# Part "a11 less a21" of a down projection, split twice: seven half-width products in place of four full ones

## The chip, the cores and the metric

One core of one Trainium2 chip runs the kernel. The metric is the device time of one execution in microseconds (us), the median over runs of the same kernel. TensorE (PE) multiplies matrices, VectorE (DVE) and ScalarE (ACT) work on elements, POOL and SP here mostly issue transfers: each has one queue of its own.

## The reference

One layer of a residual block over 2048 frames of 1024 channels: a mixer (pooling branch, convolution branch, gates, output projection) and then an MLP with a squared ReLU, everything in float32. The change touches the MLP's second product, `w_down`, and when its sums are made:

```python
D_MODEL, SEQ, D_FF = 1024, 2048, 4 * 1024
def rmsnorm(x, g):
    y = x * lax.rsqrt(jnp.mean(x * x, axis=-1, keepdims=True) + EPS)
    return y * g
...
    merged = jax.nn.sigmoid(g_a) * branch_a + jax.nn.sigmoid(g_b) * branch_b
    x = x + rmsnorm(merged @ w_o[l], norm_mix_post[l])
    h = rmsnorm(x, norm_mlp_pre[l])
    f = jnp.square(jax.nn.relu(h @ w_up[l])) @ w_down[l]
    x = x + rmsnorm(f, norm_mlp_post[l])
```

## The kernel before, in words

**Numbers in two parts.** TensorE multiplies values rounded to a shorter form (`fp32r`). So every operand is split (`split`, `parted`): ScalarE makes the high part, a rounded copy; VectorE makes the low part, the value minus that copy. A product is high by high, high by low, low by high. Weights go through `wr` (as loaded) or `ws` (a sum) to `wh` and `wl`; cells (tiles of activations, 128 x 1024 floats, 512 KB) get their parts in tiles named `big` and `tr`. `product` multiplies one weight tile with two cells in 24 matmuls of 128 x 512. In each row of them the low part of the first cell is needed at the second matmul, that of the second cell at the sixth, and the low weight at the seventh.

**Seven products for eight.** Each large product is made by a Strassen-like scheme: the two factors are cut in two by two, and seven products of sums of the pieces (numbered 1 to 7) replace eight. For the down projection parts 1, 2 and 4 have a plain piece of the weight, 3, 5, 6 and 7 a sum of pieces; part 7 has the weight a11 less a21 (blocks 0 and 2 of `w_down`). Parts 1 and 2 are cut in the same way a second time and so cost 14 half products of 24 matmuls each; the others are plain: eight jobs (s, i, b), slab s of four, token half b of two, two products of 24 each, 48 matmuls.

**The order of the down projection** (`jobs`, `items`): part 1 in seven level products (`level_product`), then part 5, part 6, part 3, part 7, part 2 in 14 halves (`level_half`), part 4, and a tail (`at_end`) with the last norm. One job of part 7, `FILL`, is made early as a filler while the output projection ends, and its result is fetched and added later. `last_product` adds a plain part's finished products into the results `c01`, `c11`, `c00` and `u`, kept in tiles `big`; four `Finish` objects take their squares and gains as the results become ready.

**What sets the order.** The program is written in the order of TensorE's work, and a compiler's list scheduler places the other engines' instructions by it. `behind()` ties what is written inside it behind the work that stands there; `tc.high_priority(offset=AHEAD)` moves it ahead. The resulting order of each engine's rows is fixed when the program is built: at run time each engine takes its rows in that order and waits where a row isn't ready. Work beside the main line is written as generators in a `Lane`, which takes so many steps of it (its rate) at each `bg()`, after each product. Two matter here. In up's second block a lane forms the weight sums of part 1's second level (`level_weights`) and then the MLP norm's squares and roots (`scales`). From the first job of part 3 on (`PREPARE`) a lane forms part 2's weight sums and cell sums (`level_weights(2, 1)`, `level_cells`); it stores them by POOL's queue (`aside`), and SP's queue (`load`) brings them back. `empty()` runs out what is left of all lanes at once.

## Time and profile before

| | before |
|---|---|
| runs | 2161.08, 2161.93, 2154.96 us; median 2161.08 |
| profiled execution | 2162.05 us, its span 2160.3 us |
| granted clock of TensorE, mean | 0.997 |
| busy: PE, DVE, ACT, POOL | 2137.6, 1688.5, 1045.0, 78.1 us |
| filler | about 1228 to 1239 us from the span's start |
| up, second block | about 1241 to 1558 us |
| part 1 (7 level products) | about 1558 to 1634 us |
| parts 5, 6, 3 | about 1634 to 1722, to 1809, to 1897 us |
| part 7 (7 jobs) | about 1897 to 1973 us |
| part 2 (14 halves) | about 1973 to 2050 us |
| part 4 | about 2050 to 2146 us |

The stages are read from the timeline of TensorE by the names of the tiles that it writes and the engines' busy time from the page's first part. A stage's windows give for each engine the busy time and, in brackets, the number of instructions; then the granted clock, the DMA engines' share and GB/s. Some matmul records are missing, so counts in a window are a few below those of the program.

### The profile page before, as it was taken

How to read it: one execution, taken by the hardware profiler on the slowest of the kernel's cores; microseconds unless marked ns; L12 is line 12 of the kernel's file. 1: busy time of each engine (PE TensorE's matmuls, PEld its weight loads, DVE VectorE, ACT ScalarE, POOL GpSimd, SP SyncE). 2: the span in 40 equal slices, each digit the busy share in tenths (PEclk: the TensorE clock that was granted, in tenths of full speed). 3: DMA queues.
4: the chain of work that ended last, by engine and by line, in shares of the span. 5: the costliest groups of instructions: out<-in, count | busy, mean ns of one | idle time of the engine just before them, and what ended most of it. 6: DMA issues, size and time to landing. Idle time of an engine off the chain costs nothing.

```text
span 2160.3 us, 25332 instructions
## 1 busy us (share of the span) xinstructions
PE 2137.6 (99%) x9585; PEld 1769.7 (82%) x9585; DVE 1688.5 (78%) x1655; ACT 1045.0 (48%) x1094; POOL 78.1 (4%) x143
## 2 busy tenths in 40 slices
PE   9999999999999999999999999999999999999998
PEld 7888888888888888888888878888888888888887
DVE  8997789998688998987858784776776657576975
ACT  6444454334543545545644674655663332234761
POOL 1000000000000000000000000000000000120002
PEclk9999999999999999999999999999999999999999
DMA  7688898777997787545787698577697997896877
GB/s 272 243 293 315 326 352 283 253 255 290 340 369 251 253 333 278 193 166 195 289 308 288 238 358 329 212 257 285 258 374 302 348 381 259 336 365 238 299 258 208
DMA packets 173930, 618.40 MB, mean 286 GB/s; under 512 B 19312, under 2 KB 21616, under 8 KB 173808
## 3 DMA queue, kind: packets, MB, share of 16 engines
q1 hardware_dynamic: 143168, 506.44, 64.4%
q0 software_dynamic: 17824, 64.07, 8.4%
q10 hardware_dynamic: 12816, 46.27, 5.5%
q8 instruction: 75, 1.23, 0.2%
q14 instruction: 47, 0.39, 0.1%
HBM read 406.89 MB, written 209.81 MB: 285 GB/s over the span
## 4 chain that ended last, share of the span: by engine, by line
PE 80%; issue 8%; DVE 6%; DMA 5%; ACT 1%; SPq 0%; POOL 0%; DVEq 0%; POOLq 0%; ACTq 0%
PE down L268 20%; PE up L268 19%; PE wo L268 8%; PE ga L268 7%; PE gb L268 7%; PE glu L268 5%; PE B L268 4%; PE rb L268 4%; PE A L268 3%; PE pool L268 3%; DVE big L121 1%; DMA fo<-w_down 1%; DVE y L1002 1%; DMA big<-fd 1%; DMA big<-x1d 1%
## 5 line engine op out<-in xcount | busy, mean ns | idle before, releaser
L268 PE MATMUL up<-big,wh 128*128 128x512 f32 x1792 | 482.7, 391 | 4.7 <-DVE big L121 2.9
L268 PEld LDWEIGHTS up<-big,wh 128*128 128x128 f32 x1792 | 337.2, 188 | 77.0 <-DVE big L121 4.1
L225 ACT CAST wh<-wr 128x1024 fp32r<-128x1024 f32 x196 | 205.9, 1051 | 308.4 <-PE up L268 90.3
L1002 DVE SCALAR_TENSOR_TENSOR y<-v,cst,y 128x1024 f32<-128x1024 f32 x240 | 307.3, 1281 | 2.8
L268 PE MATMUL down<-big,wh 128*128 128x512 f32 x872 | 295.4, 390 | 0.8 <-DVE big L121 0.8
L268 PE MATMUL up<-big,wl 128*128 128x512 f32 x896 | 277.8, 391 | 0.0
L225 ACT CAST wh<-ws 128x1024 fp32r<-128x1024 f32 x128 | 134.5, 1052 | 273.5 <-PE up L268 65.8
L268 PE MATMUL down<-big,wl 128*128 128x512 f32 x688 | 212.1, 389 | 0.0
L268 PEld LDWEIGHTS up<-big,wl 128*128 128x128 f32 x896 | 169.1, 189 | 35.1
L268 PE MATMUL down<-tr,wh 128*128 128x512 f32 x504 | 196.2, 389 | 0.5 <-DVE tr L121 0.5
L268 PEld LDWEIGHTS down<-big,wh 128*128 128x128 f32 x872 | 163.6, 188 | 35.3 <-DVE big L121 1.1
L121 DVE TENSOR_TENSOR wl<-ws,wh 128x1024 fp32r<-128x1024 f32 x120 | 146.5, 1221 | 58.5 <-ACT wh L225 58.1
L121 DVE TENSOR_TENSOR wl<-wr,wh 128x1024 fp32r<-128x1024 f32 (+1 forms) x121 | 146.3, 1210 | 28.2 <-ACT wh L225 27.8
L121 DVE TENSOR_TENSOR big<-big,big 128x1024 fp32r<-128x1024 f32 (+1 forms) x108 | 129.6, 1220 | 37.6 <-ACT big L1137 13.8
L121 DVE TENSOR_TENSOR tr<-tr,big 128x1024 fp32r<-128x1024 f32 x94 | 112.7, 1220 | 54.2 <-ACT big L1864 41.7
L268 PEld LDWEIGHTS down<-big,wl 128*128 128x128 f32 x688 | 129.1, 188 | 26.8
L268 PE MATMUL wo<-big,wh 128*128 128x512 f32 x480 | 128.5, 390 | 0.0
L268 PE MATMUL glu<-big,wh 128*128 128x512 f32 x464 | 125.3, 391 | 1.3 <-ACT big L796 0.8
L1864 ACT CAST big<-tr 128x1024 fp32r<-128x1024 f32 x70 | 72.0, 1048 | 100.0 <-DMA tr<-fd 76.7
L268 PE MATMUL gb<-big,wh 128*128 128x512 f32 x448 | 120.0, 390 | 0.0
L268 PE MATMUL ga<-big,wh 128*128 128x512 f32 x448 | 119.9, 389 | 0.0
L268 PEld LDWEIGHTS down<-tr,wh 128*128 128x128 f32 x504 | 94.6, 188 | 20.6 <-DVE tr L121 1.0
(240 smaller groups left out, 3431.6 us busy)
## 6 DMA issues: line engine op xcount, KB each, us to landing
tr<-fd SPq DMA_DIRECT2D x98, 512.0 KB, 7.8
wl<-kept SPq DMA_DIRECT2D x85, 512.0 KB, 5.0
wr<-w_down SPq DMA_DIRECT2D x80, 512.0 KB, 7.3
kept<-wl SPq DMA_DIRECT2D x72, 512.0 KB, 6.0
wr<-w_up SPq DMA_DIRECT2D x64, 512.0 KB, 4.8
wr<-w_in SPq DMA_DIRECT2D x59, 512.0 KB, 5.5
fd<-tr ACTq DMA_DIRECT2D x54, 512.0 KB, 3.9
big<-fd SPq DMA_DIRECT2D x48, 512.0 KB, 7.1
```

Source lines behind the costliest of these rows:

```text
L121: return nc.vector.tensor_tensor(o, a, b, op=ALU.subtract)
L225: nc.scalar.copy(hi[:, :n], src[:, :n])
L268: i = nc.tensor.matmul(ps, w[wp][:, (at + k) * P : (at + k + 1) * P], rhs[k][xp], start=start and n == 0, stop=stop and n == len(order) - ...
L1002: nc.vector.scalar_tensor_tensor(acc, v[:, k : k + TB], wk, acc, op0=ALU.mult, op1=ALU.add)
L1864: nc.scalar.copy(hi, t)
```

## The change

Part 7 is split a second time, as parts 1 and 2 are. Its eight jobs become 14 halves (`halves(7)`), which stand between part 6 and part 3; the order is now part 1, 5, 6, 7 (halves), 3, 2 (halves), 4. `level_half` adds their sums into `u`, and when one is complete, `u` into `c11`. The filler becomes a job of part 4. The weight sums of part 7's second level are formed by `level_weights_7`, 16 sums, in the lane of up's second block, ahead of `scales`, at rate 1.2; each loads two blocks of `w_down` by POOL's queue and stores the kept ones likewise. The cell sums are formed by `level_formed` during parts 5, 6 and the halves themselves, with loads by SP's queue. `PREPARE` stays at part 3's first job, but part 3 is now followed at once by part 2's halves, where `empty()` runs its lane out. On the whole VectorE has 40 rows more, ScalarE 16 casts more, SP's queue 10 transfers more and POOL's 34, and TensorE 48 matmuls fewer.

```diff
         kept_as(3, a12)
         yield
 
+    def level_weights_7(n):
+
+        def get(s, o):
+            t, w = fo(), fo()
+            aside(t, w_down[2 * s + o, 0])
+            aside(w, w_down[2 * s + o, 2])
+            return t, w
+
+        def kept_as(k, t):
+            level[7, k, n] = dram("level")
+            aside(level[7, k, n], t)
+
+        a21, w = get(n, 1)
+        yield
+        sub(a21, a21, w)
+        a22, s5 = get(n + 2, 1)
+        yield
+        sub(a22, a22, s5)
+        kept_as(4, a22)
+        add(s5, a21, a22)
+        kept_as(5, s5)
+        a11, s6 = get(n, 0)
+        yield
+        sub(a11, a11, s6)
+        kept_as(1, a11)
+        sub(s6, s5, a11)
+        kept_as(6, s6)
+        yield
+        sub(a21, a11, a21)
+        kept_as(7, a21)
+        a12, s3 = get(n + 2, 0)
+        yield
+        sub(a12, a12, s3)
+        kept_as(2, a12)
+        sub(s3, a12, s6)
+        kept_as(3, s3)
+        yield
...
-    SHARED, ALONE = (5, 6, 3, 7), (4,)
+    SHARED, ALONE = (5, 6, 3), (4,)
...
     jobs = [(s, i, b) for i in SHARED for s in range(SLABS) for b in range(NB)]
     jobs += [(s, i, b) for b in range(NB) for i in ALONE for s in range(SLABS)]
     END = jobs[-SLABS:]
-    FILL = (0, SHARED[-1], 0)
+    FILL = (2, ALONE[0], 0)
     jobs.remove(FILL)
...
+    formed = {}
+
+    def level_formed(p, n):
+
+        units = (2 * n, 2 * n + 1)
+
+        def get(b, u, home=TR):
+            t = mk(*home)
+            load(t, fd[b, u, "t3"])
+            return t
+
+        if p in (5, 7):
+            return [formed.pop((p, u)) for u in units]
+        made = []
+        with tc.high_priority(offset=AHEAD):
+            for u in units:
+                if p in (1, 2, 3):
+                    b, at = {1: (0, 0), 2: (0, SLABS), 3: (1, SLABS)}[p]
+                    x = get(b, u + at)
+                elif p == 4:
+                    x, t = get(0, u + SLABS), mk(*FO)
+                    load(t, fd[1, u + SLABS, "W2"])
+                    sub(x, x, t)
+                else:
+                    t3, t1, x = get(1, u), get(0, u, FO), get(1, u + SLABS, BIG)
+                    sub(t1, t3, t1)
+                    sub(t3, x, t3)
+                    sub(x, x, t1)
+                    fd[1, u + SLABS, "W2"] = o = dram("fd")
+                    aside(o, x)
+                    formed[5, u], formed[7, u] = t1, t3
+                made.append(x)
+        return made
+
     def level_parts(los, sooner=AHEAD):
 
         with tc.high_priority(offset=sooner):
...
         if n:
             k = {1: (0, 0), 2: (0, 0), 6: (0, 1), 3: (0, 1), 5: (1, 1), 7: (1, 1), 4: (1, 0)}[p]
+            c = {2: c00, 7: u}[part]
             with tc.high_priority(offset=AHEAD):
-                mark(add(c00[k], c00[k], ps))
+                mark(add(c[k], c[k], ps))
             if p in (2, 3, 7, 4):
-                fin[k[1], 0].ready[k[0]] = c00[k]
+                if part == 2:
+                    fin[k[1], 0].ready[k[0]] = c00[k]
+                else:
+                    mark(add(c11[k], c11[k], u[k]))
+                    fin[k[1], 1].ready[k[0] + 2] = c11[k]
         bg()
 
     cells = {}
@@ -2244,7 +2313,7 @@
     lanes += [Lane(1, chain)]
     filler()
     octs = mlp_up(1, parts)
-    then(lambda: lanes.extend([Lane(1, chain_of(level_weights(1, 0, fo), level_weights(1, 1, fo), scales()))]), octs[1], 1)
+    then(lambda: lanes.extend([Lane(1.2, chain_of(level_weights(1, 0, fo), level_weights(1, 1, fo), level_weights_7(0), level_weights_7(1), scales()))]), octs[1], 1)
     got = []
     then(lambda: got.append(level_loads(1, LEVEL[0], BIG)), octs[-1], 5)
     then(lambda: got.append(level_loads(1, LEVEL[1], BIG)), octs[-1], 3)
...
-    HALVES = [(p, n) for p in LEVEL for n in (0, 1)]
-    at = next(n for n, job in enumerate(jobs) if job[1] in ALONE)
-    PREPARE = (0, 3, 0)
-    items = jobs[:at] + HALVES + jobs[at:]
+    def halves(part):
+        return [("half", part, p, n) for p in LEVEL for n in (0, 1)]
+
+    early = [job for job in jobs if job[1] in (5, 6)]
+    late = [job for job in jobs if job[1] == 3]
+    items = early + halves(7) + late + halves(2) + [job for job in jobs if job[1] in ALONE]
+    starts = len(early), len(early) + 2 * len(LEVEL) + len(late)
+    ends = [at + 2 * len(LEVEL) for at in starts]
+    PREPARE = late[0]
     loads, split_of, weights = {}, {}, {}
+
+    def is_half(n):
+        return n < len(items) and len(items[n]) == 4
 
     def loads_at(n):
 
         if n < len(items) and n not in loads:
             loads[n] = True
-            if len(items[n]) == 3:
+            if not is_half(n):
                 split_of[n] = token_cells(*items[n], BIG if n < 4 else TR)
+            elif items[n][1] == 7:
+                loads[n] = level_formed(*items[n][2:])
             else:
-                p, h = items[n]
-                loads[n] = level_loads(2, p, BIG if n % 4 < 2 else TR, range(2 * h, 2 * h + 2))
+                part, p, h = items[n][1:]
+                home = BIG if n % 4 < 2 else TR
+                loads[n] = level_loads(part, p, home, range(2 * h, 2 * h + 2))
 
     def parts_at(n):
 
-        if n < len(items) and len(items[n]) == 2 and n not in split_of:
-            split_of[n] = level_parts(loads[n])
+        if is_half(n) and n not in split_of:
+            if items[n][1] == 7:
+                with tc.high_priority(offset=AHEAD):
+                    split_of[n] = [split(x, *BIG) for x in loads[n]]
+            else:
+                split_of[n] = level_parts(loads[n])
+
+    def weight_at(n):
+
+        if is_half(n) and n not in weights:
+            weights[n] = level_weight(*items[n][1:])
+
+    def sums_at(n):
+
+        for k in range(n, n + 8):
+            if is_half(k) and items[k][1:3] == (7, 6):
+                loads_at(k)
 
     for n in range(len(coming)):
         loads[n], split_of[n] = True, coming[n]
     for n, item in enumerate(items[:-SLABS]):
-        if len(item) == 2:
-            p, h = item
-            if n == at:
+        if is_half(n):
+            if n == starts[1]:
+                empty()
...
             w = weights.pop(n)
             here = split_of.pop(n)
             with behind():
                 for k in (n + 1, n + 2):
-                    if k not in weights and k < at + len(HALVES):
-                        weights[k] = level_weight(2, *items[k])
+                    weight_at(k)
                 for k in range(n + 1, n + 5):
-                    if k < at + len(HALVES) + 1:
+                    if is_half(k) or k in ends:
                         loads_at(k)
+                sums_at(n)
                 for k in (n + 1, n + 2):
                     parts_at(k)
-            level_half(p, h, w, here)
+                if n + 1 in ends:
+                    first_w = [weight_down(items[n + 1][1], items[n + 1][0], o) for o in (0, 1)]
+            level_half(*item[1:], w, here)
             continue
         s, i, b = item
-        if item == (1, 3, 0):
+        if item == PREPARE:
+            lanes.append(Lane(1.2, chain_of(level_weights(2, 1, fo), level_cells())))
+        if (s, i, b) == (0, ALONE[0], 0):
             for o in (0, 1):
                 t = fo()
                 load(t, fill[o, 0])
                 add(u[o, 0], u[o, 0], t)
-        if item == PREPARE:
-            lanes.append(Lane(1.2, chain_of(level_weights(2, 1, fo), level_cells())))
-        if (s, i, b) == (0, ALONE[0], 0):
             lanes.append(Lane(3, fin[0, 0].steps(2, 150)))
-        if n and (i in ALONE or b == 0 or (s, i) == FILL[:2]):
+        if n in ends:
+            w = first_w
+        elif n and (i in ALONE or b == 0):
             w = [weight_down(i, s, o) for o in (0, 1)]
         here = split_of.pop(n)
...
         with behind() if n < 8 else nullcontext():
             for k in (n + 1, n + 2):
-                loads_at(k)
-            if at - 2 <= n < at:
-                loads_at(n + 3)
-            if n + 1 == at:
-                parts_at(at)
-                parts_at(at + 1)
-                weights[at] = level_weight(2, *items[at])
+                if not is_half(k):
+                    loads_at(k)
+            for at in starts:
+                if at - 2 <= n < at:
+                    for k in range(at, n + 4):
+                        loads_at(k)
+                if n + 1 == at:
+                    parts_at(at)
+                    parts_at(at + 1)
+                    weight_at(at)
+            if n > 8:
+                sums_at(n)
         down_product(s, i, b, w, here)
```

What stands in the rows below: line, operation, output<-inputs, with running numbers behind the names; `down` is a finished product, `wl` a low weight, `ws` a weight sum, `fo` a tile of background work.

**Where part 3 begins, on VectorE.** Before (part 6 stands ahead of it; wl_2941 is the low part of part 3's first weight, the two adds behind it wait for a product of part 6's end):

```order
L121 TENSOR_TENSOR wl_2920_13773<-ws_2914_13764,wh_2919_13772 128x1024
L121 TENSOR_TENSOR ws_2942_13919<-wr_2943_13920,wr_2944_13922 128x1024
L121 TENSOR_TENSOR wl_2941_13916<-ws_2937_13909,wh_2940_13915 128x1024
L121 TENSOR_TENSOR ws_2969_14068<-wr_2970_14069,wr_2971_14071 128x1024
L118 TENSOR_TENSOR big_2925_13810<-big_2629_12214,down_2854_13361 128x1024
L118 TENSOR_TENSOR big_2926_13811<-big_2925_13810,big_2812_13204 128x1024
L118 TENSOR_TENSOR big_2927_13838<-big_2726_12721,down_2855_13386 128x1024
```

Now (part 7's last half stands ahead; the add with down_3018 waits for its last matmul, ws_3114 is the sum of part 3's first weight, wl_3118 its low part):

```order
L121 TENSOR_TENSOR tr_3137_14697<-tr_3137_14697,big_3138_14699 128x1024
L121 TENSOR_TENSOR tr_3139_14702<-tr_3139_14702,big_3140_14704 128x1024
L118 TENSOR_TENSOR big_2987_13948<-big_2987_13948,down_3018_14059 128x1024
L118 TENSOR_TENSOR big_2866_13350<-big_2866_13350,big_3002_14002 128x1024
L121 TENSOR_TENSOR ws_3114_14575<-wr_3115_14576,wr_3116_14578 128x1024
L121 TENSOR_TENSOR ws_3119_14585<-wr_3120_14586,wr_3121_14588 128x1024
L118 TENSOR_TENSOR big_2853_13298<-big_2853_13298,big_2987_13948 128x1024
L121 TENSOR_TENSOR wl_3118_14582<-ws_3114_14575,wh_3117_14581 128x1024
L121 TENSOR_TENSOR wl_3123_14592<-ws_3119_14585,wh_3122_14591 128x1024
```

The first weight's sum and low part stood ahead of the waiting adds and now stand behind them.

**Where part 2's first product ends, on VectorE.** Before (the add with down_3170 waits for p1's last matmul; big_3149 and big_3150 are the low parts that p2's first half takes, wl_3163 its low weight, tr_3164 and tr_3165 those of its second half):

```order
L121 TENSOR_TENSOR big_3149_15008<-big_3149_15008,big_3168_15103 128x1024
L121 TENSOR_TENSOR big_3150_15009<-big_3150_15009,big_3169_15106 128x1024
L121 TENSOR_TENSOR wl_3160_15086<-wr_3158_15083,wh_3159_15085 128x1024
L118 TENSOR_TENSOR fo_3171_15134<-fo_3171_15134,fo_3172_15138 128x1024
L121 TENSOR_TENSOR wl_3163_15092<-wr_3161_15089,wh_3162_15091 128x1024
L118 TENSOR_TENSOR big_2629_12214<-big_2629_12214,down_3170_15109 128x1024
L118 TENSOR_TENSOR fo_3171_15134<-fo_3171_15134,fo_3180_15184 128x1024
L118 TENSOR_TENSOR fo_3171_15134<-fo_3171_15134,fo_3181_15189 128x1024
L121 TENSOR_TENSOR tr_3164_15095<-tr_3164_15095,big_3178_15153 128x1024
L121 TENSOR_TENSOR wl_3175_15146<-wr_3173_15143,wh_3174_15145 128x1024
L121 TENSOR_TENSOR tr_3165_15096<-tr_3165_15096,big_3179_15156 128x1024
```

Now (the add with down_3276 waits for p1's last matmul; big_3220 is the low part of the first cell of p2's first half, that of the second follows it; the rows with two `fo` or two `big` as inputs are sums of `level_cells` and of the squares):

```order
L118 TENSOR_TENSOR big_2669_12282<-big_2669_12282,down_3276_15305 128x1024
L121 TENSOR_TENSOR fo_3229_15198<-fo_3229_15198,fo_3233_15230 128x1024
L118 TENSOR_TENSOR fo_3277_15330<-fo_3277_15330,fo_3278_15334 128x1024
L121 TENSOR_TENSOR fo_3239_15240<-fo_3239_15240,fo_3229_15198 128x1024
L121 TENSOR_TENSOR wl_3290_15393<-wr_3288_15390,wh_3289_15392 128x1024
L118 TENSOR_TENSOR fo_3277_15330<-fo_3277_15330,fo_3286_15380 128x1024
L118 TENSOR_TENSOR fo_3277_15330<-fo_3277_15330,fo_3287_15385 128x1024
L118 TENSOR_TENSOR fo_3277_15330<-fo_3277_15330 128x512
L121 TENSOR_TENSOR big_3255_15266<-big_3242_15245,big_3246_15251 128x1024
L121 TENSOR_TENSOR big_3246_15251<-big_3246_15251,big_3249_15256 128x1024
L121 TENSOR_TENSOR big_3242_15245<-big_3242_15245,big_3246_15251 128x1024
L121 TENSOR_TENSOR big_3220_15151<-big_3220_15151,big_3274_15299 128x1024
```

The low parts of the next half stood ahead of the waiting add and now stand eleven rows behind it.

**Inside part 7's halves, on VectorE**, where before there is no such place (the add with down_3064 waits for p3's last matmul; big_3104 and big_3106 are the low parts of the two cells that p4's first half takes):

```order
L121 TENSOR_TENSOR tr_3099_14469<-tr_3099_14469,big_3100_14471 128x1024
L118 TENSOR_TENSOR big_3002_14002<-big_3002_14002,down_3064_14297 128x1024
L121 TENSOR_TENSOR tr_3101_14474<-tr_3101_14474,big_3102_14476 128x1024
L121 TENSOR_TENSOR big_3104_14480<-tr_3077_14371,big_3103_14479 128x1024
L121 TENSOR_TENSOR big_3106_14484<-tr_3079_14376,big_3105_14483 128x1024
L121 TENSOR_TENSOR big_3111_14518<-tr_3088_14419,big_3110_14517 128x1024
```

One low part of other work and the two of p4 stand behind the waiting add. At the start of part 7's halves 15 rows of 128x1024 and two of 128x512 stand between the add that waits for down_2895, part 6's product for the second column and first token half, and the low weight wl_3008 of p1's second half; 78 matmuls lie between the two on TensorE.

18 lines of the change are left out of this document (5 added, 13 removed).

## The prediction

> **What bounds the kernel now.** I read the page first (shares, then the chain of waits), then the windows by stage, then the timelines of TensorE and VectorE at the few places where TensorE paused.
>
> ```profile
> span 2160.3 us, 25332 instructions
> PE 2137.6 (99%) x9585; PEld 1769.7 (82%) x9585; DVE 1688.5 (78%) x1655; ACT 1045.0 (48%) x1094; POOL 78.1 (4%) x143
> PE 80%; issue 8%; DVE 6%; DMA 5%; ACT 1%; SPq 0%; POOL 0%; DVEq 0%; POOLq 0%; ACTq 0%
> ```
>
> TensorE is busy 99% of the span and carries 80% of the chain, so the time is matmuls plus pauses of TensorE. VectorE is at 78%: a stage that gives it more rows, or gives them in a worse order, can turn the bound round.
>
> ```profile
> core 0: us, PE busy (x) PEld busy (x) DVE busy (x) ACT busy (x) POOL busy (x), PEclk, DMA share, GB/s
> 1722.00:1809.00 87.00, 87.00 (x386) 72.03 (x385) 54.48 (x47) 27.68 (x28) 3.21 (x6) 1.00 0.87 332
> 1897.00:1973.00 76.00, 76.00 (x337) 62.92 (x336) 49.62 (x45) 31.20 (x35) 8.60 (x16) 1.00 0.80 309
> 1973.00:2050.00 77.00, 76.24 (x339) 62.58 (x338) 68.94 (x75) 49.68 (x54) 5.25 (x7) 1.00 0.86 299
> ```
>
> These windows are the products of part 6, of part 7 (the seven jobs that the change replaces) and of part 2's halves. TensorE never pauses in the first two: 87.00 us hold 386 matmuls, 0.2254 us each, and 76.00 hold 337, 0.2255 each. Part 2's halves, the same kind of work that part 7 becomes, already ask VectorE for 68.94 us of 77.00.
>
> **The matmuls saved.** Part 7 had eight jobs of 48 matmuls (one of them made early as the filler); now it is 14 halves of 24, and the filler takes a job of the last part. 384 − 336 = 48 matmuls fewer, at 0.2255 us: −10.8 us. That is certain, since nothing covers TensorE.
>
> **The rule for the pauses.** VectorE takes its rows in order. A row that adds a finished product's sum waits for the product's last matmul; whatever stands behind it, such as a low part (value minus its rounded copy) that TensorE needs at once, is late by the rows between. The trace of before has one such place, in part 2's halves: VectorE's timeline, then TensorE's.
>
> ```profile
> 1983.64 1.22 DVE L118 TENSOR_TENSOR big<-big,down 128x1024 f32<-128x1024 f32 x1 [3.26 <-PE down L268]
> 1984.78 2.48 DVE L118 TENSOR_TENSOR fo<-fo,fo 128x1024 f32<-128x1024 f32 x2
> 1987.17 1.22 DVE L121 TENSOR_TENSOR tr<-tr,big 128x1024 fp32r<-128x1024 f32 x1
> 1988.31 1.22 DVE L121 TENSOR_TENSOR wl<-wr,wh 128x1024 fp32r<-128x1024 f32 x1
> 1989.44 1.22 DVE L121 TENSOR_TENSOR tr<-tr,big 128x1024 fp32r<-128x1024 f32 x1
> 1990.58 0.68 DVE L118 TENSOR_TENSOR fo<-fo 128x512 f32<-128x512 f32 x1
> 1991.18 1.22 DVE L121 TENSOR_TENSOR tr<-tr,big 128x1024 fp32r<-128x1024 f32 x1
> ...
> 1983.44 1.52 PE L268 MATMUL down<-big,wh 128*128 128x512 f32 x6
> ...
> 1990.72 0.50 PE L268 MATMUL down<-tr,wh 128*128 128x512 f32 x1 [0.55 <-DVE tr L121]
> ```
>
> The next product starts at 1983.44, the add 0.20 us later, the rows follow each other at 1.135 us (1988.31 to 1989.44) and a half-width row takes a slot of 0.60 (1990.58 to 1991.18); the fifth full row behind the add ends at 1990.66 and TensorE starts 0.06 later, having lost 0.55 us. So a pause is counted from the order: 0.20 + 1.135 per full row in front (0.60 per half row) + 1.22 for the row itself + 0.06, less the matmuls that TensorE could do meanwhile. The four places where the change builds such a queue:
>
> *Place D, part 7's first halves.* From the add of part 6's last sums of its first column (waiting for that product) to the low weight that p1's second half needs stand 15 full and 2 half rows: 0.20 + 17.03 + 1.20 + 1.22 + 0.06 = 19.7 us. TensorE has 78 matmuls meanwhile, 17.6 us. Pause 2.1. The rows are part 6's own sums, the four low parts and the six cell sums of p6, which the change makes there.
>
> *Place A, p4's first half of part 7.* Two rows stand ahead of the low part (big_3104): 0.20 + 2.27 + 1.22 + 0.06 = 3.75; TensorE needs it at its second matmul, 0.23 later: 3.5. The second cell's low part is one row later and needed four matmuls later (1.135 against 0.90): 0.2 more. Pause 3.7.
>
> *Place B, the first job of part 3.* Behind two adds stands the weight sum (ws_3114), which ScalarE must then round before any matmul.
>
> ```profile
> L225 ACT CAST wh<-ws 128x1024 fp32r<-128x1024 f32 x128 | 134.5, 1052 | 273.5 <-PE up L268 65.8
> ```
>
> 0.20 + 2.27 + 1.22 + 1.05 + 0.06 = 4.8 us to the first matmul. The low weight is the sixth row: it ends at 0.20 + 5.68 + 1.22 = 7.1, and its matmul, the seventh, would be at 4.8 + 1.35 = 6.2: 1.0 more. Pause 5.8. In before these weights stood ahead of part 6's adds.
>
> *Place C, p2's first half of part 2.* Ahead of big_3220, the low part of p2's first cell, stand the add of p1's sum, nine more full rows and a half row. 0.20 + 11.35 + 0.60 + 1.22 + 0.06 = 13.4, less 0.23, plus 0.2 for the second cell: 13.4. Before the change the same stage had both low parts ahead of the add. The new rows there are the tail of the lane that makes part 2's cells: it had 15 jobs to run in, now it has eight, and the rest is drained at the start of the stage. Its loads go out and back through POOL's queue, so C can be longer; one such store needs 7.2 us (below), and I add 2.
>
> Sum: 2.1 + 3.7 + 5.8 + 13.4 + 2 = 27.0 us. The bounds: nothing is below zero here, since nothing waits less; at the low end D and the 2 are nothing (22.9); at the high end C waits for one whole round trip (27.0 + 5.2 = 32.2).
>
> **What a pause costs beside itself.** The windows around three pauses of before, and the matmuls that ended them:
>
> ```profile
> 1280.00:1290.00 10.00, 7.87 (x27) 5.79 (x26) 9.17 (x8) 5.28 (x6) 1.06 (x2) 0.83 1.02 416
> 1473.00:1480.00 7.00, 6.48 (x21) 5.19 (x22) 5.86 (x6) 5.19 (x5) 0.00 (x0) 0.76 0.18 75
> 1655.00:1663.00 8.00, 7.24 (x32) 5.49 (x31) 3.04 (x3) 2.70 (x3) 0.00 (x0) 1.00 1.02 412
> ...
> 1282.71 1.92 PE L268 MATMUL up<-big,wh 128*128 128x512 f32 x5 [2.13 <-DVE big L121]
> 1473.52 1.65 PE L268 MATMUL up<-big,wh 128*128 128x512 f32 x6 [1.24 <-DVE tr L118]
> 1658.00 0.50 PE L268 MATMUL down<-big,wh 128*128 128x512 f32 x1 [0.76 <-DVE big L121]
> ```
>
> After the pauses of 2.13 and 1.24 us the granted clock fell to 0.83 and 0.76 of the window: 27 matmuls are worth 6.09 us and took 7.87, 21 are worth 4.74 and took 6.48. Each lost 1.8 and 1.7 us on top. After 0.76 us the clock stayed at 1.00. All four new pauses are longer than 1.24, so 4 × 1.7 = +6.8. [...]
>
> **The up block.** The change also puts 16 weight sums, 16 loads and 14 stores (through POOL's queue) into up's second block, behind the weight sums that stood there. VectorE's and TensorE's windows there, the waits from the middle of the program on, and the DMA issues of these stages:
>
> ```profile
> 1306.00:1374.00 68.00, 68.00 (x305) 56.44 (x304) 45.27 (x39) 37.27 (x37) 2.66 (x5) 1.00 0.73 271
> ...
> DVE fo L118 <- DMA fo<-w_down: 18.8, 2, 15.4
> ...
> fd<-fo POOLq DMA_DIRECT2D x22, 512.0 KB, 7.2
> level<-fo POOLq DMA_DIRECT2D x8, 512.0 KB, 5.3
> wr<-w_up SPq DMA_DIRECT2D x26, 512.0 KB, 5.1
> ```
>
> 16 rows at 1.135 are 18.2 us on top of 45.27 in 68.00: 63.5, it just fits. The DMA does not: 271 GB/s were 0.73 of its time there; by the order 23 transfers more fall into these 300 matmuls (30 new ones, 7 loads of the norm's shifted to later), 12 MB on 18.4. At the highest rate quoted, 416 GB/s, 30.4 MB take 73 us, at 271/0.73 = 371 GB/s 82: 5 to 14 us behind. VectorE takes that up as waits for loads, as it did near 1311 us for 15.4 us, which cost TensorE nothing in before: by the order up's weights were formed 131 to 148 matmuls ahead there. Now it is 101 to 124 at the fourth and fifth octets, 23 us at least. What can break it is SP's queue: a load of a sum of cells there waits for POOL's store of it, behind POOL's stores of weight sums, with the loads of w_up behind it. Price of one miss: 5.3 + 7.2 + 5.1 and the clock's 1.7, 19.3 us. Bounds 0 and 19.3; nearer 0, because a wait as long as 15.4 us was absorbed: I take 4. The other new VectorE rows (40 more in all), the 16 casts and the rest of the DMAs lie beside matmuls of stages like parts 6 and 7, whose windows leave VectorE 32.5 and 26.4 us free. Without that cover each row would be 1.135 us.
>
> **Sum**, against the profiled execution's 2162.05 us: −10.8 + 27.0 + 6.8 + 4 = +27.0, 2189.1. That execution is 1.0 above the median of the runs (2161.08), so the time to expect is 2188 us.
>
> **Rivals.** *The cover holds* (faster): the queues at A to D don't form, because ahead of each waiting add the low parts are already done. It decides from the point where the rows behind an add are fewer than TensorE's reserve (six matmuls, 1.35 us, hold one row). For it speaks part 2's stage in before, which lost just 0.55; against it the order of the rows, which is fixed at compile time. Time: 2161.1 − 10.8 = 2150. 4%. *Only the short places* (about the same): C is covered, because POOL's loads come early and the drained rows run ahead; then 2.1 + 3.7 + 5.8 and three dips of 1.7: 2161.1 − 10.8 + 16.7 = 2167. 7%. *The up block breaks* (much slower): one miss at 19.3 in place of the 4: 2203; with C at its upper end 2208. 25%; the DMA's 5 to 14 us and VectorE's 63.5 of 68 speak for it, the lead of 23 us against. [...] 10%. My sum as it stands: 54%.
>
> **How the numbers follow.** This measurement tells no change from one within 0.3%, 6.5 us: 2154.6 to 2167.6. Faster has the first rival, 4%, and 1% for what I don't see. The same has the second, whose 2167 lies at the edge: 6%. Slower takes the rest, 89%. At the low end of its bounds my sum is 2161.1 − 10.8 + 22.9 + 3 × 1.7 = 2178; the range goes on below it towards the second rival, to 2171, and up to 2212, where the up block's miss meets C's upper end and one dip more. It leaves out the first two rivals and the chance that two misses follow each other.
>
> **What would show it.** 48 matmuls fewer on TensorE. In part 7's stage (after part 6) three pauses ended by VectorE: about 2 on a low weight, about 3.7 on a low part `big`, and 4 to 6 where part 3 begins, ended by ScalarE's `wh`. One pause of 13 to 16 us 48 matmuls into part 2's halves, ended by VectorE's `big`. A granted clock under 1.00 behind each. A stage of up's second block without new pauses. I'm wrong if TensorE's pauses in the down part stay under 10 us in sum, if C is ended by a DMA rather than VectorE, or if the up block takes over 10 us more than before.

## The result

The changed kernel takes 2220.12 us (median of 4 runs, 2218.4 to 2220.52), the kernel before 2158.7 us on the same chip (4 runs, 2154.96 to 2161.93). The ratio is 1.0284, with a 95% interval of 1.0263 to 1.0304: slower by 61 us, where the prediction had 27 and its range ended at 2212. The profiled execution took 2218.4 us.

The page of the changed kernel, and its windows by stage (up's second block, part 1, parts 5 and 6, part 7's halves, part 3, part 2's halves, part 4 and the tail):

```profile
span 2216.5 us, 25437 instructions
PE 2145.3 (97%) x9537; PEld 1771.4 (80%) x9537; DVE 1735.7 (78%) x1695; ACT 1060.0 (48%) x1110; POOL 96.7 (4%) x177
```

```profile
core 0: us, PE busy (x) PEld busy (x) DVE busy (x) ACT busy (x) POOL busy (x), PEclk, DMA share, GB/s
1239.00:1573.00 334.00, 317.36 (x1385) 259.99 (x1384) 235.37 (x224) 179.43 (x186) 29.03 (x54) 0.98 0.85 318
1573.00:1659.00 86.00, 80.46 (x347) 66.38 (x346) 65.39 (x69) 48.94 (x51) 0.00 (x0) 0.96 0.76 290
1659.00:1747.00 88.00, 87.57 (x386) 72.18 (x385) 53.53 (x46) 29.05 (x30) 1.61 (x3) 1.00 0.91 347
1747.00:1834.00 87.00, 87.00 (x385) 72.08 (x384) 54.02 (x47) 26.16 (x27) 2.67 (x5) 1.00 0.89 331
1834.00:1926.00 92.00, 80.48 (x336) 64.71 (x335) 79.92 (x71) 46.01 (x46) 2.71 (x5) 0.95 0.71 263
1926.00:2016.00 90.00, 89.63 (x386) 73.96 (x387) 47.99 (x42) 22.07 (x23) 10.27 (x19) 0.97 0.79 284
2016.00:2118.00 102.00, 80.74 (x347) 65.70 (x346) 83.47 (x88) 61.69 (x70) 15.45 (x26) 0.90 0.95 349
2118.00:2208.00 90.00, 89.23 (x500) 77.77 (x500) 67.39 (x104) 37.77 (x47) 11.51 (x16) 0.98 0.74 230
```

Two stages lost the time: up's second block with the start of part 1, and the two runs of halves. Parts 5 and 6 are as they were. Taken from the first matmul of each stage to the first of the next on TensorE's timeline (up's own to its last):

| stage | before, us | changed, us | difference |
|---|---|---|---|
| up's second block and part 1 | 318.5 + 76.2 | 333.8 + 85.7 | +24.8 |
| parts 5 and 6 | 175.4 | 174.9 | −0.5 |
| parts 7, 3 and 2 | 242.1 | 284.0 | +41.9 |
| part 4 to the last matmul | 100.3 | 90.2 | −10.1 |

The sum, 56.1 us, agrees with the difference of the two spans (2216.5 − 2160.3 = 56.2). Of the 24.8 us in the first row 15.3 lie in up's block and 9.5 in part 1. Part 7 has as many matmuls in its halves as in the seven jobs of before (336); the 48 saved are those of part 4's job that is now the filler, so the saving shows in the last row, 10.1 of the 10.8 forecast.

The pauses of TensorE in part 1 and the down part, from its timeline (idle time before the row and what ended it in brackets):

```profile
1583.47 0.80 PE L586 MATMUL rb<-inv_d,fo 128*128 128x1 f32 x3 [5.54 <-DVE fo L118]
...
1840.99 1.65 PE L268 MATMUL down<-big,wh 128*128 128x512 f32 x6 [1.57 <-ACT wh L225]
1844.95 1.20 PE L268 MATMUL down<-big,wl 128*128 128x512 f32 x3 [2.31 <-DVE wl L121]
...
1908.94 0.73 PE L268 MATMUL down<-big,wh 128*128 128x512 f32 x2 [3.36 <-DVE big L121]
...
1926.37 0.80 PE L268 MATMUL down<-big,wh 128*128 128x512 f32 x1 [4.66 <-ACT wh L225]
...
2041.61 0.80 PE L268 MATMUL down<-big,wh 128*128 128x512 f32 x1 [14.89 <-ACT big L1137]
2045.55 0.80 PE L268 MATMUL down<-big,wh 128*128 128x512 f32 x1 [3.15 <-DVE big L121]
...
2117.82 0.50 PE L268 MATMUL down<-big,wh 128*128 128x512 f32 x1 [3.21 <-ACT wh L225]
```

D, A, B and C stand where the prediction put them. A and B are ended by the tiles that it named. D has a pause on a high weight (`wh`) ahead of the one on the low weight. C's long pause is ended by ScalarE's cast of `big` (L1137), and only the 3.15 us behind it by VectorE's low part, which the prediction had named. One more of B's kind, 3.21 us, stands where part 4 begins. The first row is not of the down part: the norm's last root sum, moved behind the weight sums in its lane, now falls into part 1 and holds TensorE there. That pause and the lower clock behind it (0.50 over the next 6 us) are what part 1 lost.

**How the up block lost its time.** TensorE's three longest pauses there, then VectorE's rows at the first and the last of them, then the two rows of POOL's queue that issue the loads:

```profile
1356.23 1.95 PE L268 MATMUL up<-big,wh 128*128 128x512 f32 x6 [3.24 <-DVE tr L118]
...
1390.74 2.25 PE L268 MATMUL up<-big,wh 128*128 128x512 f32 x6 [3.64 <-ACT tr L439]
...
1409.87 2.50 PE L268 MATMUL up<-big,wh 128*128 128x512 f32 x5 [6.03 <-DVE tr L118]
...
1343.01 1.23 DVE L121 TENSOR_TENSOR wl<-wr,wh 128x1024 fp32r<-128x1024 f32 x1 [0.22 <-ACT wh L225]
1352.56 2.48 DVE L121 TENSOR_TENSOR fo<-fo,fo 128x1024 f32<-128x1024 f32 x2 [8.32 <-DMA fo<-w_down]
1354.96 1.22 DVE L118 TENSOR_TENSOR tr<-up,tr 128x1024 f32<-128x1024 f32 x1
...
1406.20 2.49 DVE L121 TENSOR_TENSOR fo<-fo,fo 128x1024 f32<-128x1024 f32 x2 [8.28 <-DMA fo<-w_down]
1408.60 1.22 DVE L118 TENSOR_TENSOR tr<-up,tr 128x1024 f32<-128x1024 f32 x1
...
1342.69 0.55 POOL L131 DMA_DIRECT2D fo<-w_down x1
...
1393.09 0.55 POOL L131 DMA_DIRECT2D fo<-w_down x1
```

At 1344.2 VectorE's next row is a weight sum whose load was issued at 1342.69 and landed at 1352.43. VectorE stands for 8.32 us; behind the sums waits `tr<-up`, the row that takes up's finished product out of its accumulator, and TensorE, which needs that accumulator, stops for 3.24. At 1409.87 the same again, with a load issued at 1393.09, landed at 1406.17. The pause of 3.64 has the same origin by one more step: VectorE's sums had waited 5.00 us for a block of `w_down` until 1380.31, its later rows came late by that, and ScalarE's copy out of the accumulator (`tr<-up`, L439) stood behind a cast that waited for one of them. Loads of `w_up` did not hold TensorE: no pause here ends on a `wr` load or its cast. One, of 1.45 us at 1382.73, ends on a low weight of up (`wl`), and that row too stood directly behind the sum at 1380.31.

### The profile page after: what moved, and what is told of

Its sections match the earlier page's. It is cut to its first block, busy times and chain, and to the rows that moved or that the text cites. A ratio compares the mean times of both kernels' runs of the same rounds, so it can differ in the third digit from the quotient of the medians.

```text
span 2216.5 us, 25437 instructions
## 1 busy us (share of the span) xinstructions
PE 2145.3 (97%) x9537; PEld 1771.4 (80%) x9537; DVE 1735.7 (78%) x1695; ACT 1060.0 (48%) x1110; POOL 96.7 (4%) x177
## 5 line engine op out<-in xcount | busy, mean ns | idle before, releaser
L268 PEld LDWEIGHTS up<-big,wh 128*128 128x128 f32 x1792 | 338.0, 189 | 89.1 <-DVE tr L118 10.1
L225 ACT CAST wh<-wr 128x1024 fp32r<-128x1024 f32 x210 | 220.6, 1052 | 354.0 <-PE up L268 65.8
L268 PE MATMUL down<-big,wh 128*128 128x512 f32 x992 | 324.9, 398 | 31.3 <-ACT big L1137 14.9
L268 PEld LDWEIGHTS down<-big,wh 128*128 128x128 f32 x992 | 190.8, 193 | 74.8 <-ACT big L1137 15.3
L225 ACT CAST wh<-ws 128x1024 fp32r<-128x1024 f32 x118 | 124.1, 1053 | 248.4 <-DVE ws L121 94.9
L268 PE MATMUL down<-big,wl 128*128 128x512 f32 x704 | 221.2, 396 | 2.3 <-DVE wl L121 2.3
L121 DVE TENSOR_TENSOR wl<-wr,wh 128x1024 fp32r<-128x1024 f32 (+1 forms) x135 | 163.2, 1212 | 48.4 <-ACT wh L225 48.0
L121 DVE TENSOR_TENSOR wl<-ws,wh 128x1024 fp32r<-128x1024 f32 x110 | 134.2, 1222 | 64.4 <-ACT wh L225 64.2
L268 PE MATMUL down<-tr,wh 128*128 128x512 f32 x416 | 163.3, 393 | 0.0
L121 DVE TENSOR_TENSOR tr<-tr,big 128x1024 fp32r<-128x1024 f32 x80 | 95.4, 1221 | 44.5 <-ACT big L1897 36.6
L268 PEld LDWEIGHTS wo<-big,wh 128*128 128x128 f32 x480 | 89.9, 188 | 18.9 <-ACT tr L1378 0.4
```

What stands on the lines that cost most here:

```text
L121: return nc.vector.tensor_tensor(o, a, b, op=ALU.subtract)
L225: nc.scalar.copy(hi[:, :n], src[:, :n])
L268: i = nc.tensor.matmul(ps, w[wp][:, (at + k) * P : (at + k + 1) * P], rhs[k][xp], start=start and n == 0, stop=stop and n == len(order) - ...
```

## Experiments

The measure for the up block is the time of up's second block (first to last matmul) plus part 1 (first matmul to part 5's first): 394.7 us before, 419.5 changed. A time given without a number of runs is one execution. How far the measure repeats is seen in e5, e6 and e10 below, which leave these stages as they are in the changed kernel: 417.9, 419.3 and 419.9 us. Of the edits the lines that matter are shown, the lane's line cut down to its `Lane`; the letters A to D are the prediction's.

### What the sums cost, and by which way

**Without the sums, loads and stores** (e1):

```diff
-    Lane(1.2, chain_of(level_weights(1, 0, fo), level_weights(1, 1, fo), level_weights_7(0), level_weights_7(1), scales()))
+    Lane(1, chain_of(level_weights(1, 0, fo), level_weights(1, 1, fo), scales()))
...
```

> The changed kernel without the 16 weight sums of part 7's second level and their 16 loads and 14 stores (this part of the computation is left out: its halves take plain blocks of w_down), the lane of up's second block again at rate 1. The measure is the time of up's second block and part 1 together, 394.7 us in the kernel before and 419.5 in the changed one. Every theory of the up block that blames these sums expects 394 to 399 us here, so about 2195 in all, and part 7's halves (92.5) and part 2's (102.2) as they are. If up and part 1 stay above 410, the cause is the shift of the norm's steps or something that I don't name.

Measured: 2183.59 us (one run; the kernel before 2153.86 beside it), up and part 1 388.4, part 7 90.9, part 2 102.4. So everything that the up block and part 1 lost comes from these sums, with their loads and stores and the shift of the norm's steps behind them: 31 us, 6 more than the comparison with before shows, since even the pauses of before (2.13 and 1.24 with their slow matmuls) are gone in this execution. Part 1 takes 76.2 us again. The down part is as in the changed kernel.

**Without the stores** (e2):

```diff
-            level[7, k, n] = dram("level")
-            aside(level[7, k, n], t)
+            pass
...
```

> The changed kernel with the 16 loads and 16 sums of part 7's weights, but without the 14 stores of the sums (left out: the halves take plain blocks of w_down). Theory 1, the ring: a load of a weight block waits for a tile whose store has to be issued behind VectorE's sum and to land first, so VectorE meets loads that were issued too late; without stores the tiles come free at the sum, VectorE's waits for fo<-w_down (26.8 us in the changed kernel) fall under 10 and up with part 1 takes 395 to 403 us. Theory 2, the DMA's capacity: about half of the added bytes are gone, so about half of the 24.8 us, 405 to 410. Theory 3, VectorE's 16 rows themselves: 415 to 420, since the rows are all there.

Measured: 2195.33 us, up and part 1 397.0. Theory 3 falls: all 16 rows of VectorE are there. The ring is where it was expected, VectorE's waits for these blocks too (7.3 us). Of the 8.6 us above the kernel without the sums, 6.8 are part 1's (83.0 us), so 16 sums and 16 loads without stores cost the up block itself less than 2.

**The kernel before with idle transfers** (e4):

```diff
+    def copies():
+        for n in range(16):
+            for s in range(2):
+                aside(dram("idle"), w_down[2 * (n % 4) + s, n // 4])
+            yield
-    Lane(1, chain_of(level_weights(1, 0, fo), level_weights(1, 1, fo), scales()))
+    Lane(1, chain_of(level_weights(1, 0, fo), level_weights(1, 1, fo), scales())), Lane(1.2, when_idle(copies(), 8))
```

> The kernel before, with 32 transfers of 512 KB (blocks of w_down copied within DRAM) issued by POOL's queue over the same part of up's second block; no instruction waits for them. Theory 2, the DMA's capacity, expects up's weights and cells to come late as in the changed kernel: up with part 1 at 405 to 420 us in place of 394.7. Theories 1 and 3 expect 394 to 399, the total within 5 us of the kernel before.

Measured: 2174.95 us (before: 2153.86), up and part 1 406.3, with one pause of 14.09. Its rows, TensorE's and VectorE's, and the window ahead of it:

```profile
1368.45 2.08 PE L268 MATMUL up<-big,wh 128*128 128x512 f32 x4 [14.09 <-DVE tr L118]
...
1366.04 1.23 DVE L118 TENSOR_TENSOR ws<-wr,wr 128x1024 f32<-128x1024 f32 x1 [15.26 <-DMA wr<-w_up]
...
1330.00:1350.00 20.00, 20.00 (x90) 16.57 (x89) 8.52 (x8) 10.07 (x10) 2.08 (x5) 1.00 1.02 409
```

With nobody to wait for them the copies went out in bursts of up to seven, the DMA was full (1.02), and a load of w_up came 15 us late, again at VectorE's head and ahead of `tr<-up`. So bytes alone can do it when they come in bursts, which theory 1 had not allowed for.

**Copies in place of the stores** (e7): the same bytes, without the wait for VectorE.

```diff
-            level[7, k, n] = dram("level")
-            aside(level[7, k, n], t)
+            aside(dram("idle"), w_down[2 * n, k % 4])
...
```

> The changed kernel with each of the 14 stores of a weight sum replaced by a copy of 512 KB within DRAM, issued at the same place of POOL's queue, for which no instruction waits and which doesn't wait for VectorE (left out: the sums reach no weight, the halves take plain blocks of w_down). Up's second block with part 1 takes 419.5 us in the changed kernel, 397.0 without the stores, 388.4 without sums, loads and stores. The ring (a load waits for a tile whose store is issued behind VectorE's sum and has to land) expects 390 to 404, though as many bytes move as in the changed kernel. The DMA's capacity expects 410 to 422, and by the copies of the earlier run, which came in bursts, a single pause of over 8 us would speak for it as well.

Measured: 2209.75 us, up and part 1 412.8, in the band of the DMA's capacity. VectorE's wait for these loads fell from 26.8 us (changed kernel) to 15.3 (this one), both between 1240 and 1600 us; the row of this one:

```profile
DVE fo L121 <- DMA fo<-w_down: 15.3, 6, 7.3
```

Of the 22.5 us that leaving the stores out saved, the ring (the tile that its store keeps) holds 6.7 and the bytes 15.8, if a copy within DRAM weighs on the other loads as a store does. That isn't shown: the copies took 11.5 us to land (median), the stores of the changed kernel 5.8, so 15.8 may well be too much for the stores. My theory 1 falls as the only cause.

**The lane slower, a sum two steps behind its loads** (e12):

```diff
-    Lane(1.2, chain_of(level_weights(1, 0, fo), level_weights(1, 1, fo), level_weights_7(0), level_weights_7(1), scales()))
+    Lane(0.7, chain_of(level_weights(1, 0, fo), level_weights(1, 1, fo), level_weights_7(0), level_weights_7(1)))
...
         a21, w = get(n, 1)
-        yield
+        yield 2
...
+        if n == 0:
+            lanes.append(Lane(1.2, scales()))
```

> The changed kernel with the lane of up's second block at rate 0.7 without the norm's steps (these start with part 5 instead), and each weight sum written two steps behind its loads in place of one: the same 16 loads, 16 sums and 14 stores, spread over the rest of the block. If the order is what costs (a sum is placed too few matmuls behind its load, whose 8.7 us VectorE then waits out ahead of the rows that free up's product), up with part 1 takes 386 to 393 us (419.5 in the changed kernel, 388.4 without the sums). If the added bytes cost by themselves, 400 to 410. Parts 5, 6 and 7 take 5 to 15 us more, from the norm's steps put there.

Measured: 2220.8 us; up and part 1 398.2, between the two bands and 9.8 above the kernel without the sums. So this takes away two thirds of the cost, but by two changes at once: 9.5 us are part 1's (76.2 again), where the norm's last sum no longer falls, and 11.8 the up block's, where the same transfers are spread. VectorE no longer waits for blocks of `w_down` there; the three pauses that are left (3.01, 2.60 and 4.47 us) each follow a wait of VectorE for a load of w_up (4.55, 6.90 and 4.67 us) directly ahead of `tr<-up`. The norm's steps, moved on, cost 25 us more than in the changed kernel in parts 6 and 7 (102.6 against 87.0, and 102.1 against 92.6), and the total is where it was.

**The sums on POOL** (e15):

```diff
     def level_weights_7(n):
+        def sub(o, a, b):
+            return nc.gpsimd.tensor_tensor(o, a, b, op=ALU.subtract)
+        def add(o, a, b):
+            return nc.gpsimd.tensor_tensor(o, a, b, op=ALU.add)
```

> The changed kernel with the 16 weight sums done by POOL in place of VectorE: the same loads, stores, tiles and places in the lane, but VectorE never waits for them (a sum of half width takes POOL 1.26 us in the kernel before, so about 2.5 each, in POOL's queue between the loads and the stores). If VectorE's standing at these sums ahead of the rows that free up's product is the way from late loads to TensorE, up with part 1 takes 388 to 397 us (419.5 in the changed kernel). If the bytes themselves make up's own weights late, 405 to 415. If a store of cells that now stands in POOL's queue behind the sums holds SP's queue, a pause ended by a load of w_up or of cells appears, and 420 or more.

Measured: 2218.8 us, up and part 1 419.1, no better at all. The waits there:

```profile
POOL fo L1781 <- DMA fo<-w_down: 37.1, 6, 9.8
...
DVE fo L121 <- DMA fo<-fd: 19.7, 1, 19.7
...
PE up L268 <- DVE wl L121: 11.5, 1, 11.5
```

The waits of SP's queue between 1370 and 1412 us:

```profile
SPq L127 <- DMA level<-fo: 20.7, 3, 14.9
```

VectorE waits no more for part 7's weight blocks there (its one long wait of before, for part 1's, is still there with 14.9 us); POOL does, 37.1 us, and behind it in POOL's queue stand its stores of weight sums. SP's queue stood 14.9 us, until 1388.74, before it issued the load of a cell: by the trace until one of these stores (`level<-fo`) had landed. VectorE stood 19.7 us at that cell, and up's low weight behind it held TensorE for 11.5. That is near the third branch of the expectation (419.1 where it said 420 or more), though what SP waited for was a store of a weight sum and not of a cell; why the load waits for that store the trace doesn't say. The first branch, 388 to 397 us, missed. Since another queue jammed in its stead, the run doesn't test the way by VectorE in the changed kernel. It shows that the queue that takes the sums in order makes late what stands behind them.

What these six runs leave open is how much is the bytes' and how much the order's. With the bytes added, loads take longer: those of w_up took 4.7 us (median) to land in this stretch (1290 to 1420 us) in the kernel before, 7.9 in the changed one. But the version below with the lane at rate 1.4, which has the same sums, loads and stores, moves more in this stretch (46.79 MB against 43.90) and loses 13 us, not 31; VectorE's waits for the blocks of `w_down` fall from 26.8 to 8.5 us in it. The DMA issues of before, of the changed kernel, and the totals of the changed kernel and of that version:

```profile
wr<-w_up SPq DMA_DIRECT2D x15, 512.0 KB, 4.7
```

```profile
DMA packets 12044, 43.90 MB, mean 338 GB/s; under 512 B 1340, under 2 KB 1340, under 8 KB 12038
...
wr<-w_up SPq DMA_DIRECT2D x12, 512.0 KB, 7.9
```

```profile
DMA packets 12843, 46.79 MB, mean 360 GB/s; under 512 B 1436, under 2 KB 1436, under 8 KB 12836
```

So in the changed kernel the bytes don't explain it by themselves, though in bursts they can (e4). I read it so: longer loads are the means, and the order decides which row of VectorE stands at the head when one is late. Why the faster lane meets its loads with less waiting stays open.

### The four places of the down part

**C: the lane of part 2's sums begun at the third half of part 7** (e5):

```diff
-    PREPARE = late[0]
+    PRE = 2
...
+            if n == starts[0] + PRE:
+                lanes.append(Lane(1.2, chain_of(level_weights(2, 1, fo), level_cells())))
...
-        if item == PREPARE:
-            lanes.append(Lane(1.2, chain_of(level_weights(2, 1, fo), level_cells())))
```

> The changed kernel with the lane that makes part 2's weight sums and cell sums begun at the third half of part 7 in place of part 3's first job, so that nothing of it is left to run out at the start of part 2. My theory of place C (VectorE's rows of that lane stand between the add of p1's sum and the low part that p2 needs) expects the pause of 14.9 us to go, part 2's halves to fall from 102.2 us to 80 to 86, and part 7's halves to grow by 0 to 6 us from the rows moved there: total 2200 to 2207. The rival, that the loads of the cells through POOL's queue or the fin squares on ScalarE are what p2 waits for, expects a pause of 8 us or more to stay in part 2.

Measured: 2192.55 us (before: 2153.86); the pauses of 14.89 and 3.15 are gone, part 2 takes 81.3 us in place of 102.2, part 7 88.2 in place of 92.6 and part 3 91.7 in place of 89.3. Parts 7, 3 and 2 fall by 22.8. The rival falls as it was worded; but the edit moves the lane's loads and stores along with its rows of VectorE, so it can't tell the two apart. The rows that moved cost nothing in part 7 and 2.4 us in part 3.

In the changed kernel the place looks like this: VectorE's rows from the add on, then ScalarE's:

```profile
2026.83 1.21 DVE L118 TENSOR_TENSOR big<-big,down 128x1024 f32<-128x1024 f32 x1
2027.96 1.22 DVE L121 TENSOR_TENSOR fo<-fo,fo 128x1024 f32<-128x1024 f32 x1
...
2036.29 1.23 DVE L121 TENSOR_TENSOR wl<-wr,wh 128x1024 fp32r<-128x1024 f32 x1 [4.84 <-ACT wh L225]
2037.43 2.55 DVE L118 TENSOR_TENSOR fo<-fo,fo 128x1024 f32<-128x1024 f32 x2
2040.02 0.69 DVE L118 TENSOR_TENSOR fo<-fo 128x512 f32<-128x512 f32 x1
...
2035.21 1.04 ACT L225 CAST wh<-wr 128x1024 fp32r<-128x1024 f32 x1 [6.51 <-DMA wr<-level]
2036.16 2.00 ACT L754 ACTIVATE fo<-big 128x1024 f32<-128x1024 f32 x2
2038.07 2.55 ACT L796 ACTIVATE big<-big,cst 128x512 f32<-128x512 f32 x4
2040.52 3.88 ACT L1137 CAST big<-big 128x1024 fp32r<-128x1024 f32 x4
```

The queue on VectorE is the one forecast. It is lengthened by a wait of 4.84 us, because ScalarE stood 6.51 us at the load of the next weight; the cell's cast, which TensorE's first matmul needs, comes behind that weight, two squares and four gains. Both pauses less that wait are 13.2 us, close to the 13.4 that the prediction counted for the rows (an estimate: it takes the wait to have put off all that stands behind it by its whole length).

**B: part 3's first weights one half earlier** (e6):

```diff
-                if n + 1 in ends:
-                    first_w = [weight_down(items[n + 1][1], items[n + 1][0], o) for o in (0, 1)]
+                if n + 2 in ends:
+                    first_w = [weight_down(items[n + 2][1], items[n + 2][0], o) for o in (0, 1)]
```

> The changed kernel with the first weights of part 3 formed one half of part 7 earlier. My theory of place B (the weight's sum stands behind the adds that wait for p4's last matmul) expects the pause of 4.66 us at the start of part 3 and the slow matmuls behind it to go: part 7 and part 3 together 181.9 us now, 173 to 177 here, the pause inside p4 (3.36) and the one of 14.9 in part 2 as they are. A rival, that part 7's halves as a whole give VectorE more than it can do, expects the pause to move somewhere into part 7 or part 3 and the sum to stay above 179.

Measured: 2212.64 us (before: 2155.1), parts 7 and 3 174.9 us in place of 181.9, the pause gone, and the 3.21 us at the start of part 4 with it (part 2 with that pause: 99.4 in place of 102.2).

**A: low parts one half earlier** (e10):

```diff
-                for k in (n + 1, n + 2):
+                for k in (n + 1, n + 2) + ((n + 3,) if item[1] == 7 and is_half(n + 3) and items[n + 3][1] == 7 and n + 3 in loads else ()):
                     parts_at(k)
```

> The changed kernel with the low parts of part 7's cells made one half earlier. My theory of place A (the low part that p4's first half needs stands behind the add of p3's sum) expects the pause of 3.36 us and its slow matmuls to go and part 7's halves with the pause behind them to take 86 to 89 us instead of 92.5; the pause where part 3 begins (4.66) stays or shrinks a little. A rival, that VectorE is simply behind at that point, expects a pause of 2 us or more to stay in p4, and the same sum.

Measured: 2210.99 us (before: 2155.1); the pause of 3.36 is gone, part 7 with the pause behind it takes 87.1 in place of 92.6, and B's pause is 4.72.

### All together

**A, B and C undone, the lane at rate 1.4** (e11):

```diff
-    Lane(1.2, chain_of(level_weights(1, 0, fo), level_weights(1, 1, fo), level_weights_7(0), level_weights_7(1), scales()))
+    Lane(1.4, chain_of(level_weights(1, 0, fo), level_weights(1, 1, fo), level_weights_7(0), level_weights_7(1), scales()))
```

and the edits of e5, e6 and e10.

> The changed kernel, whole, with what undoes A, B and C (low parts one half earlier, part 3's first weights one half earlier, the lane of part 2's sums begun at the third half of part 7) and the lane of up's second block at rate 1.4 in place of 1.2. If the three places are independent costs of the order of the rows, part 7, part 3 and part 2 together take 250 to 258 us (284.0 in the changed kernel, 242.1 in the one before with its 48 matmuls more), and with the up block as it is the time is about 2220 less 28, 2192. If the faster lane also lets VectorE meet its loads later and fewer at a time, up with part 1 falls from 419.5 to 400 to 410 and the time to 2172 to 2182. The rival, that VectorE's 40 rows more are too many for these stages wherever they stand, expects over 2200.

Measured: 2164.52 us (8 runs, 2160.02 to 2172.36) against 2155.1 (11 runs); ratio 1.0045, interval 1.0026 to 1.0064. Up and part 1 take 401.5, parts 7, 3 and 2 246.9. Both bands held or were passed: 37 us less in the three stages, 18 in the up block, where the rate is the only edit. It is still slower than before.

**The same with D undone and the sums left out** (e13): `range(n, n + 8)` in `sums_at` becomes `range(n, n + 10)`, and the lane and the plain blocks are those of e1.

> The kernel with A, B and C undone, and D too (part 7's cell sums begun ten jobs ahead in place of eight), and with the 16 weight sums, their loads and their stores left out (the halves take plain blocks of w_down): what the change would be worth if the sums cost nothing. By the 48 matmuls less, 10.8 us, and by what the runs without sums showed of up and part 1 (388.4 against 394.7 in the profile of before), 2155.1 less 10 to 17: 2138 to 2145. If 14 halves need more VectorE than they have, wherever the rows stand, over 2150.

Measured: 2154.17 us (10 runs) against 2157.55 (15 runs); ratio 0.9985, interval 0.9975 to 0.9995: faster by 3.4 us, not by 10 to 17. Up and part 1 take 390.5, part 4 90.8, as hoped, but part 6 now takes 92.4 (87.0 before), where D's rows went, and part 3 90.1 (87.0), where the lane of C ends. Part 7's halves themselves run through in 76.6 us, with VectorE nearly full:

```profile
1811.00:1888.00 77.00, 76.87 (x339) 63.37 (x338) 72.87 (x64) 42.12 (x43) 7.10 (x14) 1.00 0.91 338
```

**Half of the sums in part 5** (e14), the other half in the up block at rate 1.2, A to D undone (against e11, with the range of e13):

```diff
-    Lane(1.4, chain_of(level_weights(1, 0, fo), level_weights(1, 1, fo), level_weights_7(0), level_weights_7(1), scales()))
+    Lane(1.2, chain_of(level_weights(1, 0, fo), level_weights(1, 1, fo), level_weights_7(0), scales()))
...
+        if n == 0:
+            lanes.append(Lane(0.8, level_weights_7(1)))
```

> The whole kernel with A, B, C and D undone as before, and only the first half of the weight sums in up's second block (rate 1.2), the second half in a lane of part 5 (rate 0.8). If both halves find room for their 8 loads and 7 stores, up with part 1 takes 386 to 394 us, part 5 loses 0 to 6 us, parts 7, 3 and 2 together take 238 to 244, and the time is 2142 to 2152, below the 2155.1 of the kernel before. If the bytes that the change adds cost their time wherever they stand, 2155 to 2165, as in the version with all sums in the up block (2164.5).

Measured: 2171.44 us (5 runs), ratio 1.0069, interval 1.0056 to 1.0082. Up and part 1 take 397.0, part 5 93.2, part 6 97.2; parts 7, 3 and 2 are in the band with 242.5. Up and part 1 missed their band, and parts 5 and 6 lost 6.2 and 10.2 us; of the latter e13, without any sums, has 5.4. The time lies 6 us beyond the second expectation's band, the bytes that cost their time wherever they stand. It fits that expectation better than the first, and doesn't prove it.

**The sums on POOL, A, B and C undone** (e16): the edits of e15, e5, e6 and e10, the lane at rate 1.2.

> The whole kernel with A, B and C undone and the 16 weight sums done by POOL, the lane at rate 1.2. If the sums on POOL bring up and part 1 to 388 to 397 us, then with parts 7, 3 and 2 as in the version with all three undone (246.9 us) the time is 2145 to 2155; if POOL's queue holds others, 2165 or more.

Measured: 2183.3 us (5 runs), ratio 1.0131, interval 1.0113 to 1.0149; up and part 1 416.8. POOL's queue holds the others, as in e15.

No whole version tried beats the kernel before; the one that does leaves the sums out.

## Why the prediction was wrong

The direction was right, and so were the places in the down part; the size was not, and the time lies 8 us above the range. (The range's upper end should have been 2210 by its own terms: 2203 + 5.2 + 1.7.) Of the prediction's three signs of being wrong the last came true: the up block took over 10 us more. Against the terms of the sum (profiled executions):

| term | forecast, us | measured, us |
|---|---|---|
| 48 matmuls | −10.8 | −10.1 |
| D | 2.1 | 1.57 + 2.31 |
| A | 3.7 | 3.36 |
| B | 5.8 | 4.66 |
| C | 13.4 + 2 | 14.89 + 3.15 |
| start of part 4 | not seen | 3.21 |
| slow matmuls behind D, A, B, C | 6.8 | 1.7 + 1.7 + 2.1 + 2.3 |
| up block and part 1 | 4 | 24.8 |

**The step that failed** is the term of the up block: "nearer 0, because a wait as long as 15.4 us was absorbed: I take 4". It measured 24.8 (15.3 in the up block, 9.5 in part 1), or 31 against the kernel without the sums. It was mis-sized, and the ground for it was wrong too. The step looked at how far up's weights are formed ahead of their use (101 to 124 matmuls), and asked what could make a weight late. VectorE's waits for weight blocks reached TensorE by a shorter way: the row that empties up's accumulator stood behind the waiting sum, and TensorE had run out of work 3 to 6 us before that row came. That the one long wait of before cost nothing was a matter of where it fell. The same row stood directly behind it there:

```profile
1311.42 1.23 DVE L118 TENSOR_TENSOR fo<-fo,fo 128x1024 f32<-128x1024 f32 x1 [15.43 <-DMA fo<-w_down]
1312.56 1.22 DVE L118 TENSOR_TENSOR tr<-up,tr 128x1024 f32<-128x1024 f32 x1
```

But the three products that were emptied during that wait were ScalarE's to empty (at 1296.27, 1301.71 and 1307.15 us, 5.44 apart), so VectorE's turn came only about when its wait ended. The step also had the sign of the trouble in hand, the 12 MB that put the DMA "5 to 14 us behind", and counted it as absorbed. And the shift of the norm's steps into part 1, worth a pause of 5.54 there and 9.5 us in all, was named as a shift and priced at nothing.

**The rival "the up block breaks"** (25%, 2203 to 2208) had the sign, one miss where there were five pauses (3.24, 1.45, 3.64 and 6.03 us in the up block, 5.54 in part 1), and another mechanism: SP's queue held by the store of a cell sum. No run shows it in that form; the nearest is e15, where SP's queue was held by a store of a weight sum.

**The rule for the pauses** held. Counting rows between a waiting add and what TensorE needs gave A within 0.3 us and B within 1.1. e10, e6 and e5 took away A, B and C one at a time by moving those rows (in e5 with their lane's loads and stores), and the pauses went with them. C was 2.6 longer than forecast: the round trip that I allowed 2 us for was a load of a weight, at ScalarE's head, and so the long pause ended on ScalarE's cast. D came in two steps, a high weight from ScalarE ahead of the low one that I had counted. Part 4's start has the same arrangement as part 3's, and the prediction left it out.

**The clock.** After each of the four places TensorE ran on at a lower clock (0.72, 0.72, 0.62 and 0.60 in the rows below), as after two pauses of before (0.83 and 0.76). The windows of 6 us behind a pause of 1.45 us in the up block, which cost nothing more, and behind D, A, B and C (TensorE's busy time less 0.2255 us for each matmul gives the loss in the table):

```profile
1383.00:1389.00 6.00, 4.10 (x18) 3.03 (x17) 4.66 (x5) 2.39 (x3) 1.53 (x3) 1.00 0.86 352
...
1845.00:1851.00 6.00, 6.00 (x19) 4.79 (x20) 5.10 (x5) 4.17 (x5) 0.00 (x0) 0.72 0.92 345
1909.00:1915.00 6.00, 6.00 (x19) 4.51 (x20) 6.00 (x6) 0.51 (x1) 0.00 (x0) 0.72 0.75 236
1926.30:1932.30 6.00, 5.93 (x17) 4.66 (x18) 5.75 (x6) 2.08 (x4) 0.00 (x0) 0.62 0.93 338
2045.50:2051.50 6.00, 5.95 (x16) 4.75 (x17) 4.54 (x4) 0.00 (x0) 0.53 (x1) 0.60 1.00 346
```

After D's second pause, 2.31 us, the clock was 0.72, and after A, 3.36 us, 0.72 as well. But the prediction's rule, that each pause longer than 1.24 us is paid twice, isn't general: the pause of 1.45 us was followed by 1.00, and in e1 the second pause of D was 3.19 us long, and the clock behind it was 1.00 (last section).

**The deeper reason, as far as it is known.** The stage that was plain left VectorE 26 us free (49.62 of 76.00, in the prediction's windows); as halves it takes 72.87 of 77.00 in e13, with the rows of part 2's lane among them, and 79.92 of 92.00 in the changed kernel. So the 10.8 us of matmuls were bought with a stage in which VectorE has little left, and rows that have to be somewhere move to its neighbours: in e13 to part 6 and part 3, in e14 to parts 5 and 6. Why they cost time there stays open. Room on VectorE wasn't what part 6 of e13 lacked (busy 58.62 of 92.00 us): ahead of the pause of 2.84 that ends on ScalarE's `wh`, ScalarE had stood 10.68 us at the load of a cell, and that weight's sum had waited 1.76 us for a load on VectorE.
